# A hybrid decoder layer on one core: more products by the seven-product scheme, and an order of instructions worked out in rounds

## The chip, the core and the metric

The kernel runs on one NeuronCore of one Trainium2 chip. The metric is the device time of one launch in microseconds; of several runs the median is given. Engines: PE (TensorE, matrix products), DVE (VectorE), ACT (ScalarE), POOL (GpSimd, here mostly an issuer of accumulating DMAs), SP (SyncE, here the issuer of loads and stores), and 16 DMA engines behind all queues. PE writes into PSUM, which has 8 banks.

## What is computed

One layer for 256 tokens of width 2048, in float32, all weights read once from HBM:

```python
h = rmsnorm(x, g_mix); proj = h @ w_in            # 2048 x 15872
x_r, g_r, q, k, v, gate_r, gate_a = split(proj)   # 2816, 2816, then 2048 each
y_r = (gelu(g_r) * rg_lru(conv4(x_r))) @ w_rnn_out
y_a = stick_breaking_attention(norm(q), norm(k), v) @ w_attn_out   # 16 heads of 128
x = x + (sigmoid(gate_r) * y_r + sigmoid(gate_a) * y_a) @ w_o
g, u = split(rmsnorm(x, g_ffn) @ w_ffn_gu)        # 2 x 5632
x = x + (silu(g) * u) @ w_ffn_down
x = x + sigmoid(rmsnorm(x, g_ple) @ w_ple_gate) * (p @ w_ple_proj)
```

rg_lru is a gated linear recurrence over the tokens whose two gates come from 16 block-diagonal 176 x 176 products each.

## The kernel before, in words

**A product.** Every float32 operand is split into two float32r tiles, hi (a copy on ACT) and lo = value - hi (a subtraction on DVE), and `prod` (lines 202 to 214) runs three matmuls: hi x hi, hi x lo, lo x hi. Token tiles are the stationary side (128 x 128), weights the moving side (512 columns). A weight tile of 128 x 1024 (512 KB) is loaded by SP into `raw`, and `weights` makes `whi` and `wlo` of it.

**Groups.** `group` computes two blocks of 512 output columns for 256 tokens, over all k tiles of 128, in four PSUM banks (q). A plain k tile costs one weight tile and 4 products. Some k tiles are taken in pairs by a seven-product scheme (Strassen's, in Winograd's form): rows are the two k tiles of a pair, columns the two blocks of outputs, token halves the other side. Two pairs stand side by side in one tile, so a block of two pairs has seven weight tiles of 128 x 1024 ("11", "22", "21", and the sums T1 to T4) and 2 products for each, 14 where plain work has 4 weight tiles and 16 products. T1 = w11 + w12 and T3 = w22 + w12 are made by an accumulating DMA that POOL issues onto the raw tile (`add`), after its old content was split; T2 and T4 are added on DVE. Four of the seven go through a fifth bank (u), whose content is copied out by ACT (ja, jc, jd) and combined on DVE (je); at the end `join` adds those to the four banks. The token side needs, for each such pair, sums of its four quarters (`half_sums`: four small DVE operations and one split).

**Stages.** xr/gr in 6 groups (column blocks of the recurrent branch, with conv, gates, scan as hooks between k tiles of later groups), ro (2 groups), gtr, v, q and k, gta (gate of the attention branch), ao (attention output), wo, then the FFN: 11 gu groups and three rounds of dn over 16, 16 and 12 k tiles (order gu 0 to 3, dn, gu 4 to 7, dn, gu 8 to 10, dn), and pg (the last gate). The table `CFG` lists which pairs go by seven: 130 over all groups, none in ao.

**Gates.** `gates` (line 786 and on) puts the recurrence gate of two 128-column tiles into one PSUM bank, one half each, and the input gate's into another. ACT reads each half by a sigmoid as soon as the planner sees that half complete.

**The planner.** `build` records every operation with an engine, a duration, a latency and what it reads and writes; no instruction is issued yet. `deadlines` gives each a due time, back from the moment PE would use it. `schedule` then runs a clock over the five engines: among the ready operations PE takes the first in program order within a window of 60, the others the one due first, and each takes a buffer if there is one. There are 42 buffers of 128 x 1024 (L), 22 of 128 x 512 (H) and the 8 banks (P). A tile gets the buffer that has been free longest. The order of starts is the order in which `emit` writes the instructions; on the chip every engine runs its own list in that order, and semaphores hold true dependences.

Of the kernel before, what the change touches and what calls it, by code (L numbers as in the profile page):

```python
# [75 lines left out]
class Op:  # L76
    __slots__ = ("eng", "dur", "lat", "emit", "deps", "succ", "tiles", "due", "at", "n", "left", "ready",
                 "start", "table", "name", "cap", "acc", "reads", "size", "early")
# [9 lines left out]
class Program:  # L88
# [72 lines left out]
    def act(self, o, i, f, scale=None, bias=None, accum=None, name="", **kw):  # L161
        n = o.b - o.a
        reads, args = [i], {}
        for k, v in (("scale", scale), ("bias", bias)):
            if isinstance(v, Ref):
                reads.append(v)
        np_ = len(reads) - 1
        writes = [o] + ([accum] if accum is not None else [])

        def emit(nc):  # L170
            kw = {}
            for k, v in (("scale", scale), ("bias", bias), ("accum_out", accum)):
                if v is not None:
                    kw[k] = v.ap() if isinstance(v, Ref) else v
            nc.scalar.activation(o.ap(), i.ap(), f, **kw)  # L175
        d = 0.05 + 0.000875 * n + 0.09 * np_ + (0.2 if accum is not None else 0)
        return self.op("ACT", d, 0.15, emit, reads, writes, table=f, name=name, **kw)
# [60 lines left out]
LOAD_US, ADD_US, DMA_LEAD, DMA_TAIL = 1.575 / 512, 2.96 / 512, 1.3, 1.2  # L238
# [6 lines left out]
def deadlines(prog):  # L245
    for o in prog.ops:
        o.succ = []
    for o in prog.ops:
        for d in o.deps:
            d.succ.append(o)  # L250
    for o in reversed(prog.ops):
        if o.eng == "PE":
            o.due = o.at
            continue
        fin = o.at + (40.0 if o.cap is None else o.cap)
        if o.cap is None and any(r.t.kind == "P" for r in o.reads):
            fin = o.at + 2.5
        for s in o.succ:
            fin = min(fin, s.due)
        o.due = fin - o.lat - o.dur  # L260
        if o.size:
            o.due -= DMA_LEAD + DMA_TAIL + dma_us(o.size)


def schedule(prog, room, window, lag=0.0):
# [4 lines left out]
    deadlines(prog)  # L270
    for o in prog.ops:
        o.left = len(o.deps)
# [8 lines left out]
    free = {k: [(0.0, i) for i in range(n)] for k, n in room.items()}  # L281
# [31 lines left out]
    while left or events:  # L313
        moved = True
        while moved:
            moved = False
            for e in ready:
# [71 lines left out]
        while events and events[0][0] <= now + 1e-9:  # L389
# [7 lines left out]
            for t in o.tiles:  # L397
                t.left -= 1
                if t.left == 0 and t.kind in room:
                    heapq.heappush(free[t.kind], (now, t.slot))  # L400
    prog.span = now
    return sorted(prog.ops, key=lambda o: (o.start, o.n))

# [49 lines left out]
FQ = [16, 16, 12]  # L453


def order_of(ks, nd, lead=0):
# [7 lines left out]
    first, second = ("11", "22", "T1", "21"), ("T2", "T3", "T4")  # L464
    blocks = [[(m, d) for d in range(nd)] for m in (*first, *second)]
    n = len(ks)
    end = max(1, round(n / 7))
    rest = n - end
    out = blocks[0] + blocks[1]
    for i, b in enumerate(blocks[2:]):  # L470
        take = round(rest * (i + 1) / 5) - round(rest * i / 5)
        out += [ks.pop(0) for _ in range(take)]
        out += b
    return out + ks


def build(cfg):
# [31 lines left out]
    for n in ("h", "l"):  # L509
# [3 lines left out]
        w1t.append(t)  # L513

# [83 lines left out]
    def raw_of(tiles, name="raw"):  # L598
# [3 lines left out]
        return t, c  # L602

    def wslot(tiles):
        t, c = raw_of(tiles)
        return weights(t, c)
# [7 lines left out]
    def group(w, cols, ks, pairs, sums, tokens, how, hooks=None, lead=0):  # L614
# [16 lines left out]
        for n, x in enumerate(order):  # L631
# [10 lines left out]
            if m in ("11", "22", "21"):  # L642
                r, b = {"11": (0, 0), "21": (1, 0), "22": (1, 1)}[m]
                chain[m, dp] = raw_of(src(r, b, dp), "r" + m)[0]
# [3 lines left out]
            if m in ("T1", "T3"):  # L648
                if how(m) == "dma":
                    pr.add(raw.all, chain["b12", dp], 512, name="add")  # L650
                else:
# [4 lines left out]
            if m in ("T2", "T4"):  # L656
# [62 lines left out]


    xg, xsum = [], {}
    xp = cfg["x"]
# [63 lines left out]
    def gates(p):  # L786
# [31 lines left out]
        for e in range(2):  # L818
            s = slice(e * 256, e * 256 + 256)
            pr.vec(330, (lambda r, a, i: lambda nc: nc.vector.tensor_tensor_scan(r.ap(), a.ap(), i.ap(), 0.0, ALU.mult,  # L820
# [4 lines left out]
    def finish(p):  # L825
# [6 lines left out]
        if p in cfg["ro"]:  # L832
            ysum[p] = half_sums(r, "ys")

    def how(m):
        return "dma"

    def xr_group(b, n, hooks):
        c = [cols_of(C_XR + 4 * b, n), cols_of(C_GR + 4 * b, n)]
        if n == 4:  # L840
            out = group("in", c, range(KD), cfg["xr"][b], xsum, xg, cfg["how"], hooks, cfg["lead"] if b == 0 else 0)
# [75 lines left out]
    for g in range(2):  # L917
# [3 lines left out]
        for x in group("ro", c, range(KR), cfg["ro"], ysum, LazyPairs(y), cfg["how"], hooks):  # L921
# [9 lines left out]
    for g in range(2):  # L931
        c = [cols_of(C_GTR + 8 * g), cols_of(C_GTR + 8 * g + 4)]
        for n, x in enumerate(group("in", c, range(KD), cfg["gtr"], xsum, xg, cfg["how"])):
# [9 lines left out]
    for g in range(2):  # L943
        c = [cols_of(C_V + 8 * g), cols_of(C_V + 8 * g + 4)]
        for n, x in enumerate(group("in", c, range(KD), cfg["v"], xsum, xg, cfg["how"])):
# [7 lines left out]
    heads = {}  # L953
# [98 lines left out]
    def att_o(hp):  # L1052
# [16 lines left out]
        ost.append(split(ps.all, "ost"))  # L1069
# [24 lines left out]
    nq, ng = slots(KD, cfg["qk"]), slots(KD, cfg["gta"])  # L1094
    first = spread(att_hooks(range(4), cfg["att0"], cfg["every"], cfg["at"]), [nq, nq, ng, ng])
    second = spread(att_hooks(range(4, 8), cfg["att0"], cfg["every"], cfg["at"]), [ng, ng, 99])
# [5 lines left out]
    def qk(which, c0, g, hooks):  # L1102
        c = [cols_of(c0 + 8 * g), cols_of(c0 + 8 * g + 4)]
        head_norms(which, g, group("in", c, range(KD), cfg["qk"], xsum, xg, cfg["how"], hooks))
# [6 lines left out]
    for g in range(2):  # L1111
        c = [cols_of(C_GTA + 8 * g), cols_of(C_GTA + 8 * g + 4)]
        for n, x in enumerate(group("in", c, range(KD), cfg["gta"], xsum, xg, cfg["how"], hk[2 + g])):
# [9 lines left out]
    osum = {}  # L1123
    if cfg["ao"]:
        raise NotImplementedError
    mix, msum = {}, {}

    def next_mix(p):
        def run():
# [6 lines left out]
            if p in cfg["wo"]:  # L1136
# [15 lines left out]
    for g in range(2):  # L1152
        c = [cols_of(8 * g), cols_of(8 * g + 4)]
        for n, x in enumerate(group("ao", c, range(KD), cfg["ao"], osum, ost, cfg["how"], take(cfg["turn"]))):
# [34 lines left out]
    for g in range(2):  # L1189
        c = [cols_of(8 * g), cols_of(8 * g + 4)]  # L1190
        out = group("wo", c, range(KD), cfg["wo"], msum, mix, cfg["how"], take(cfg["turn"]))
# [7 lines left out]
        for p in range(4 * g, 4 * g + 4):  # L1199
            pend.append(next_h(hg, hsum, p, PC_GF, cfg["gu"], "hg"))  # L1200
# [7 lines left out]
    dn_pairs = {p for v in cfg["dn"] for p in v}  # L1208

    def gu(g):  # L1210
        c = [cols_of(4 * g), cols_of(44 + 4 * g)]
        out = group("gu", c, range(KD), cfg["gu"], hsum, hg, cfg["how"], take(cfg["turn"][:len(pend)]))
# [28 lines left out]
    def down(q, g):  # L1241
        c = [cols_of(8 * g), cols_of(8 * g + 4)]
        out = group("dn", c, range(f0[q], f0[q] + FQ[q]), cfg["dn"][q], asum, acts, cfg["how"],
# [6 lines left out]
        if q == len(FQ) - 1:  # L1250
            for p in range(4 * g, 4 * g + 4):
                pend.append(next_h(h3, sum3, p, PC_GP, cfg["pg"], "h3"))
# [14 lines left out]
    for g in range(2):  # L1267
        c = [cols_of(8 * g), cols_of(8 * g + 4)]
        out = group("pg", c, range(KD), cfg["pg"], sum3, h3, cfg["how"], take(cfg["turn"][:len(pend)]))
# [21 lines left out]
class LazyPairs:  # L1291


    def __init__(self, pairs):
        self.pairs = pairs

    def __getitem__(self, i):
        return self.pairs[i]
# [10 lines left out]
def make():  # L1309
    pr = build(CFG)  # L1310
    return pr, schedule(pr, ROOM, WINDOW)
# [78 lines left out]
```

## Time and profile before

| | |
|---|---|
| median of 3 runs | 1877.42 us (1877.06 to 1879.14) |
| the profiled execution | 1874.15 us |
| its span in the trace | 1872.4 us |
| PE, DVE, ACT busy | 98%, 86%, 68% of the span |
| loads, accumulating DMAs | 50.7%, 20.2% of 16 DMA engines' time |

How to read it: a wait is listed as *engine, waiting tile and line, <- engine and instruction that ended it: total us, times, longest*. A row of groups lists *line engine operation out<-in (shape) xcount | busy us, mean ns of one | idle before, releaser*. A stretch row gives *from:to, its length, then busy us (and count) of PE, PE's weight loads, DVE, ACT and POOL, the clock granted to PE, the mean share of the DMA engines that is busy, GB/s*. In a timeline "x6" merges six like instructions in a row, from the first one's start to the last one's end. A matmul's own duration overlaps the next one's; its spacing from start to start is what a product costs.

### The profile page before, as it was taken

The numbers are of one execution on the slowest core, as the hardware profiler recorded it, in microseconds if no ns is written. First come the engines' busy times: TensorE is split into PE (matmuls) and PEld (weight loads), VectorE is DVE, ScalarE is ACT, GpSimd is POOL, SyncE is SP. The second block draws the span as 40 slices with busy tenths as digits, with TensorE's granted clock in tenths as the row PEclk, the third lists the DMA queues.
The fourth block names the chain that finished last, engine by engine and source line by source line (L and its number), as shares of the span: only waits on it lengthen the run. The fifth ranks groups of instructions, "written<-read, shape, count | busy, mean of one in ns | idle before, by whom it ended". The sixth has DMA issues, their size and how long they took to land. (4 is left out here: it accounts for less than half of the span.)

```text
span 1872.4 us, 23719 instructions
## 1 busy us (share of the span) xinstructions
PE 1832.8 (98%) x8478; PEld 1523.6 (81%) x8478; DVE 1602.2 (86%) x1887; ACT 1277.0 (68%) x1696; POOL 115.5 (6%) x139
## 2 busy tenths in 40 slices
PE   8899999999999999999999999999999999999998
PEld 7678778888888888888888888888878888787887
DVE  7998998988888778888668889888898889898995
ACT  7798989856566677878645676666566656665773
POOL 0000000001000000000000000000100010000000
PEclk9999999999999999999999999999999999999999
DMA  9665665678877665656657777778877788777673
GB/s 368 199 188 184 191 186 177 190 238 262 240 229 230 206 191 162 188 170 236 205 168 221 221 205 206 200 217 243 262 202 205 225 220 265 209 215 246 194 226 103
DMA packets 112294, 397.52 MB, mean 212 GB/s; under 512 B 12592, under 2 KB 12976, under 8 KB 112176
## 3 DMA queue, kind: packets, MB, share of 16 engines
q1 hardware_dynamic: 93312, 327.84, 50.7%
q0 software_dynamic: 18720, 68.17, 20.2%
q8 instruction: 66, 1.08, 0.2%
q14 instruction: 52, 0.43, 0.1%
q10 hardware_dynamic: 144, 0.01, 0.0%
HBM read 393.86 MB, written 2.10 MB: 211 GB/s over the span
## 5 line engine op out<-in xcount | busy, mean ns | idle before, releaser
L175 ACT ACTIVATE shi<-r 128x1024 fp32r<-128x1024 f32 x455 | 472.7, 1054 | 250.6 <-DMA r<-in_w_dram 117.6
L142 DVE TENSOR_TENSOR slo<-r,shi 128x1024 fp32r<-128x1024 f32 x455 | 546.7, 1218 | 112.7 <-ACT shi L175 98.9
L142 DVE TENSOR_TENSOR wlo<-raw,whi 128x1024 fp32r<-128x1024 f32 (+2 forms) x418 | 499.7, 1206 | 60.8 <-ACT whi L175 49.5
L175 ACT ACTIVATE whi<-raw 128x1024 fp32r<-128x1024 f32 (+2 forms) x418 | 431.5, 1045 | 129.0 <-DMA raw<-in_w_dram 47.6
L210 PE MATMUL q<-whi,xg 128*128 128x512 f32 x624 | 245.4, 393 | 6.1 <-ACT xg L175 6.1
L211 PE MATMUL q<-wlo,xg 128*128 128x512 f32 x624 | 244.2, 391 | 2.5 <-DVE wlo L142 2.4
L212 PE MATMUL q<-whi,xg 128*128 128x512 f32 x624 | 243.9, 391 | 0.0
L188 POOL DMA_DIRECT2D r<-in_w_dram x130 | 113.4, 872 | 1704.3 <-DVE slo L142 853.0
L142 DVE TENSOR_TENSOR r<-r,r 128x1024 f32<-128x1024 f32 x130 | 157.9, 1219 | 1.2
L210 PEld LDWEIGHTS q<-whi,xg 128*128 128x128 f32 x624 | 117.8, 189 | 29.9 <-ACT xg L175 6.1
L211 PEld LDWEIGHTS q<-wlo,xg 128*128 128x128 f32 x624 | 117.8, 189 | 27.3 <-DVE wlo L142 3.6
L210 PE MATMUL q<-whi,hg 128*128 128x512 f32 x352 | 139.0, 395 | 0.0
L211 PE MATMUL q<-wlo,hg 128*128 128x512 f32 x352 | 138.1, 392 | 0.0
L212 PE MATMUL q<-whi,hg 128*128 128x512 f32 x352 | 137.8, 392 | 0.0
L212 PEld LDWEIGHTS q<-whi,xg 128*128 128x128 f32 x624 | 117.7, 189 | 24.7
L212 PEld LDWEIGHTS q<-whi,hg 128*128 128x128 f32 x352 | 66.8, 190 | 14.1
L211 PEld LDWEIGHTS q<-wlo,hg 128*128 128x128 f32 x352 | 66.8, 190 | 13.7
L210 PEld LDWEIGHTS q<-whi,hg 128*128 128x128 f32 x352 | 66.7, 190 | 13.6
L210 PE MATMUL q<-whi,act 128*128 128x512 f32 x192 | 75.6, 394 | 0.0
L211 PE MATMUL q<-wlo,act 128*128 128x512 f32 x192 | 74.9, 390 | 0.0
L212 PE MATMUL q<-whi,act 128*128 128x512 f32 x192 | 74.8, 390 | 0.0
L175 ACT ACT_TABLE_LOAD x52 | 66.7, 1283 | 2.2 <-PEq L1377 1.2
(412 smaller groups left out, 3719.0 us busy)
## 6 DMA issues: line engine op xcount, KB each, us to landing
raw<-in_w_dram SPq DMA_DIRECT2D x396, 512.0 KB, 4.5
r<-in_w_dram SPq DMA_DIRECT2D x195, 512.0 KB, 4.7
r<-in_w_dram POOLq DMA_DIRECT2D x130, 512.0 KB, 7.5
raw<-in_w_dram SPq DMA_DIRECT2D x16, 448.0 KB, 4.0
xq<-in_x_dram SPq DMA_DIRECT2D x8, 256.0 KB, 8.0
x<-in_x_dram SPq DMA_DIRECT2D x8, 256.0 KB, 6.7
xt<-in_xT_dram SPq DMA_DIRECT2D x7, 256.0 KB, 8.4
raw<-in_w_dram SPq DMA_DIRECT2D x4, 320.0 KB, 4.9
```

The lines of the kernel that those rows point to most:

```text
L142: return self.vec(n, lambda nc: nc.vector.tensor_tensor(o.ap(), a.ap(), b.ap(), op), [a, b], [o], name=name, **kw)
L175: nc.scalar.activation(o.ap(), i.ap(), f, **kw)
L188: return self.op("POOL", 0.85, 0.0, lambda nc: nc.gpsimd.dma_start(o.ap(), src(nc), accum_op=ALU.add), [], [o], size=-kb, name=name)
L210: nc.tensor.matmul(ps.ap(), x[0].ap(), w[0].ap(), start=start, stop=False, **kw)
L211: nc.tensor.matmul(ps.ap(), x[0].ap(), w[1].ap(), start=False, stop=False, **kw)
L212: nc.tensor.matmul(ps.ap(), x[1].ap(), w[0].ap(), start=False, stop=stop, **kw)
```

## The change

1. `CFG`: 184 pairs by seven instead of 130. gtr and v go from 4 pairs to 6 a group, q, k and gta from 2 to 4, ao from 0 to 4, wo from 2 to 4, ten of the gu groups from 4 to 6, the second pg group from 4 to 6. In q, k, gta and ao T4 too is made by an accumulating DMA (from w21, read again) instead of DVE. Token sums are made for the pairs that any group uses; the attention output gets a copy (h) for it.
2. `order_of`: the seven-product steps are spread differently among the plain k tiles.
3. In a PSUM bank an operation of another engine now depends on all recorded PE operations on the bank, whatever half they touch, and the other way round.
4. Nine matmuls on constants (warm) ahead of the first product.
5. A load issued by SP takes the buffer freed last; all else the one free longest, as before.
6. The planner's costs: ACT's are split by PSUM and SBUF source, the scan's is raised, loads are due 5 us earlier, and data counts as seen 0.5 us (loads) or 2 us (accumulating DMAs) later.
7. `improve` runs `schedule` 20 times. After each it looks, for every gap of PE in its own clock, back along the chain that ended last, and makes those operations due earlier by up to 3 us. The order of the round with the shortest planned run is used.

```diff
-                    if overlap(a, b, r.a, r.b):
+                    if overlap(a, b, r.a, r.b) or (t.kind == "P" and (eng == "PE") != (p.eng == "PE")):
...
-                        t.slot = heapq.heappop(free[t.kind])[1]
+                        if o.eng == "SP":
+                            i = max(range(len(free[t.kind])), key=lambda i: free[t.kind][i][:2])
+                        else:
+                            i = 0
+                        _, t.slot, o.why = free[t.kind].pop(i)
...
-                    seen = server + DMA_TAIL
+                    seen = server + DMA_TAIL + (LATE if o.size < 0 else LATE / 4)
...
+def improve(prog, room, window, rounds, gain=1.0):
+    boost, best, kept = {}, None, {}
+    for _ in range(rounds):
+        order = schedule(prog, room, window, boost)
+        if best is None or prog.span < best:
+            best, kept = prog.span, dict(boost)
...
+            x, n = o, 0
+            while x is not None and n < 40:
+                d = max(x.deps, key=lambda d: (d.start + d.dur + d.lat, d.n), default=None)
+                if d is None or d.start + d.dur + d.lat < x.start - 0.6:
+                    d = x.why if x.why is not None else d
+                if d is None or d.eng == "PE":
+                    break
+                add[d.n] = max(add.get(d.n, 0.0), min(gap, 3.0))
+                x, n = d, n + 1
+        for n, v in add.items():
+            boost[n] = boost.get(n, 0.0) + gain * v
+    order = schedule(prog, room, window, kept)
+    return order
...
+    cuts = [round(n * f) for f in SPREAD]
+    p = [ks[i:j] for i, j in zip([0] + cuts, cuts + [n])]
+    s = {m: [(m, d) for d in range(nd)] for m in ("11", "22", "T1", "21", "T2", "T3", "T4")}
+    h = (nd + 1) // 2
+    return (s["11"] + s["22"] + p[0] + s["T1"] + s["21"][:h] + p[1] + s["T2"] + s["21"][h:] + p[2] + s["T3"] + p[3]
+            + s["T4"] + p[4])
...
+    warm = tile("warm", "P")
+    pr.mms([(warm.all, ones_r.all, w1t[0].all, 0.4, True, True) for _ in range(9)], [ones_r.all, w1t[0].all], [warm.all],
+           name="warm")
+    pr.pe = 0.0
...
-CFG = dict(lead=8, x=[4, 5, 6, 7], xr=[[6, 7]] + [[4, 5, 6, 7]] * 4, ro=[0, 1, 2, 3], gtr=[4, 5, 6, 7], v=[4, 5, 6, 7], qk=[4, 5], gta=[4, 5],
-           ao=[], wo=[0, 1], gu=[0, 1, 2, 3], dn=[[0, 1, 2, 3], [8, 9, 10, 11], [16, 17]], pg=[0, 1, 2, 3],
-           how=lambda m: "dma", att0=4, every=9, at=(0, 4, 10, 16), turn=[4, 5, 6, 7])
+F4, F6, X4, X6 = [0, 1, 2, 3], [0, 1, 2, 3, 4, 5], [4, 5, 6, 7], [2, 3, 4, 5, 6, 7]
+LATER = ("T1", "T3", "T4")
+CFG = dict(xr=[[6, 7]] + [X4] * 4, ro=[F4] * 2, gtr=[X6] * 2, v=[X6] * 2, qk=[X4] * 4, gta=[X4] * 2, ao=[F4] * 2,
+           wo=[F4] * 2, gu=[F4] + [F6] * 10, dn=[[F4] * 2, [[8, 9, 10, 11]] * 2, [[16, 17]] * 2], pg=[F4, F6],
+           how=dict(qk=LATER, gta=LATER, ao=LATER), lead=8, att0=4, every=9, at=(0, 4, 10, 16), turn=[4, 5, 6, 7])
```

The program that comes out has 162 matmuls of products fewer and the nine warming ones more, 27 loads fewer (621 DMAs of SP instead of 648) and 70 accumulating DMAs more (200 instead of 130).

More of the change, by code (lines that the diff above doesn't have):

```diff
@@ L77 @@
     __slots__ = ("eng", "dur", "lat", "emit", "deps", "succ", "tiles", "due", "at", "n", "left", "ready",
-                 "start", "table", "name", "cap", "acc", "reads", "size", "early")
+                 "start", "why", "table", "name", "cap", "acc", "reads", "size", "early")
 def overlap(a, b, c, d):
@@ L175, in emit @@
             nc.scalar.activation(o.ap(), i.ap(), f, **kw)
-        d = 0.05 + 0.000875 * n + 0.09 * np_ + (0.2 if accum is not None else 0)
+        d = (0.03 + 0.000875 * n if i.t.kind == "P" else 0.094 + 0.000832 * n) + 0.09 * np_ + (0.13 if accum is not None else 0)
         return self.op("ACT", d, 0.15, emit, reads, writes, table=f, name=name, **kw)
@@ L261, in deadlines, with schedule @@
         if o.size:
-            o.due -= DMA_LEAD + DMA_TAIL + dma_us(o.size)
-def schedule(prog, room, window, lag=0.0):
+            o.due -= DMA_LEAD + DMA_TAIL + SPARE + dma_us(o.size)
+        if boost:
+            o.due -= boost.get(o.n, 0.0)
+def schedule(prog, room, window, boost=None):
     import bisect
     import heapq
-    deadlines(prog)
+    deadlines(prog, boost)
     for o in prog.ops:
-        o.left = len(o.deps)
+        o.left, o.why = len(o.deps), None
     wait = {}
@@ L280, in schedule @@
         wait[k].sort()
-    free = {k: [(0.0, i) for i in range(n)] for k, n in room.items()}
+    free = {k: [(0.0, i, None) for i in range(n)] for k, n in room.items()}
     pes = [o for o in prog.ops if o.eng == "PE"]
@@ L399, in schedule @@
                 if t.left == 0 and t.kind in room:
-                    heapq.heappush(free[t.kind], (now, t.slot))
+                    bisect.insort(free[t.kind], (now, t.slot, o), key=lambda x: x[:2])
     prog.span = now
     return sorted(prog.ops, key=lambda o: (o.start, o.n))
+def improve(prog, room, window, rounds, gain=1.0):
[4 more added lines that the diff above has]
+            best, kept = prog.span, dict(boost)
+        end = 0.0
+        add = {}
+        for o in order:
+            if o.eng != "PE":
+                continue
+            gap = o.start - end
+            end = o.start + o.dur
+            if gap < 0.05:
+                continue
+            x, n = o, 0
[11 more added lines that the diff above has]
+    return order
 def emit(prog, order, nc, tc, pools):
@@ L453 @@
 FQ = [16, 16, 12]
+SPREAD = (0.3, 0.5, 0.65, 0.8)
 def order_of(ks, nd, lead=0):
@@ L463, in order_of @@
         return ks[:lead] + order_of(ks[lead:], nd)
-    first, second = ("11", "22", "T1", "21"), ("T2", "T3", "T4")
-    blocks = [[(m, d) for d in range(nd)] for m in (*first, *second)]
     n = len(ks)
[L467 to L474, printed above, removed]
+    cuts = [round(n * f) for f in SPREAD]
[4 more added lines that the diff above has]
+            + s["T4"] + p[4])
 def build(cfg):
@@ L601, in raw_of @@
         pr.load(t[:c], src, c // 2, name=name)
-        return t, c
+        return t, src
     def wslot(tiles):
-        t, c = raw_of(tiles)
-        return weights(t, c)
+        return weights(raw_of(tiles)[0], P * len(tiles))
     def part(w, a, n):
@@ L647, in group @@
             raw = chain["22" if m in ("22", "T3") else "21" if m == "21" else "11", dp]
[L648 to L651, printed above, removed]
+            if m in how:
+                s_ = {"T1": "b12", "T3": "b12", "T2": "b22", "T4": "b21"}[m]
+                pr.add(raw.all, chain[s_, dp], 512, name="add")
+            elif m in ("T1", "T3"):
+                if True:
                     if ("r12", dp) not in chain:
@@ L718, in token_scales, with hw, union @@
         rsqrt_mean(r.all, v[:2], D)
+    def hw(stage, g):
+        h = cfg["how"].get(stage, ("T1", "T3"))
+        return h[g] if isinstance(h, list) else h
     xg, xsum = [], {}
-    xp = cfg["x"]
+    def union(*keys):
+        return sorted({p for k in keys for v in cfg[k] for p in v})
+    xp = union("xr", "gtr", "v", "qk", "gta")
     for i in range(NPD):
@@ L831, in finish @@
         y.append(split(r.all, "y"))
-        if p in cfg["ro"]:
+        if p in union("ro"):
             ysum[p] = half_sums(r, "ys")
-    def how(m):
-        return "dma"
     def xr_group(b, n, hooks):
@@ L840, in xr_group @@
         if n == 4:
-            out = group("in", c, range(KD), cfg["xr"][b], xsum, xg, cfg["how"], hooks, cfg["lead"] if b == 0 else 0)
+            out = group("in", c, range(KD), cfg["xr"][b], xsum, xg, hw("xr", b), hooks, cfg["lead"] if b == 0 else 0)
             for i, x in enumerate(out):
@@ L920, in build @@
                           (8, lambda: finish(8)), (11, lambda: finish(9)), (15, finish_last)]) if g == 0 else None
-        for x in group("ro", c, range(KR), cfg["ro"], ysum, LazyPairs(y), cfg["how"], hooks):
+        for x in group("ro", c, range(KR), cfg["ro"][g], ysum, y, hw("ro", g), hooks):
             if x[1] is None:
@@ L932, in build @@
         c = [cols_of(C_GTR + 8 * g), cols_of(C_GTR + 8 * g + 4)]
-        for n, x in enumerate(group("in", c, range(KD), cfg["gtr"], xsum, xg, cfg["how"])):
+        for n, x in enumerate(group("in", c, range(KD), cfg["gtr"][g], xsum, xg, hw("gtr", g))):
             o = join(x, "gt")
@@ L944, in build @@
         c = [cols_of(C_V + 8 * g), cols_of(C_V + 8 * g + 4)]
-        for n, x in enumerate(group("in", c, range(KD), cfg["v"], xsum, xg, cfg["how"])):
+        for n, x in enumerate(group("in", c, range(KD), cfg["v"][g], xsum, xg, hw("v", g))):
             o = join(x, "v")
@@ L950, in build @@
             vs.append(v)
-    heads = {}
+    heads, osum = {}, {}
     qs, ks_, zst, ost = {}, {}, {}, []
@@ L1068, in att_o @@
         pr.mms(jobs, reads, [ps.all], name="o")
-        ost.append(split(ps.all, "ost"))
+        if hp in union("ao"):
+            h = tile("h", "H")
+            act(h.all, ps.all, AF.Copy, name="h")
+            ost.append(split(h.all, "ost"))
+            osum[hp] = half_sums(h, "os")
+        else:
+            ost.append(split(ps.all, "ost"))
     steps = (att_t, att_z, att_e, att_o)
@@ L1092, in slots @@
         return nk - 2 * len(pairs) + 7 * (len(pairs) // 2)
-    nq, ng = slots(KD, cfg["qk"]), slots(KD, cfg["gta"])
-    first = spread(att_hooks(range(4), cfg["att0"], cfg["every"], cfg["at"]), [nq, nq, ng, ng])
-    second = spread(att_hooks(range(4, 8), cfg["att0"], cfg["every"], cfg["at"]), [ng, ng, 99])
+    nq, ng = [slots(KD, v) for v in cfg["qk"][2:]], [slots(KD, v) for v in cfg["gta"]]
+    first = spread(att_hooks(range(4), cfg["att0"], cfg["every"], cfg["at"]), nq + ng)
+    second = spread(att_hooks(range(4, 8), cfg["att0"], cfg["every"], cfg["at"]), ng + [99])
     hk = [first[0], first[1], first[2], first[3], {}]
@@ L1102, in qk @@
     def qk(which, c0, g, hooks):
+        n = 2 * g + (which == "k")
         c = [cols_of(c0 + 8 * g), cols_of(c0 + 8 * g + 4)]
-        head_norms(which, g, group("in", c, range(KD), cfg["qk"], xsum, xg, cfg["how"], hooks))
+        head_norms(which, g, group("in", c, range(KD), cfg["qk"][n], xsum, xg, hw("qk", n), hooks))
     qk("q", C_Q, 0, None)
@@ L1112, in build @@
         c = [cols_of(C_GTA + 8 * g), cols_of(C_GTA + 8 * g + 4)]
-        for n, x in enumerate(group("in", c, range(KD), cfg["gta"], xsum, xg, cfg["how"], hk[2 + g])):
+        for n, x in enumerate(group("in", c, range(KD), cfg["gta"][g], xsum, xg, hw("gta", g), hk[2 + g])):
             o = join(x, "ga")
@@ L1153, in build @@
         c = [cols_of(8 * g), cols_of(8 * g + 4)]
-        for n, x in enumerate(group("ao", c, range(KD), cfg["ao"], osum, ost, cfg["how"], take(cfg["turn"]))):
+        for n, x in enumerate(group("ao", c, range(KD), cfg["ao"][g], osum, ost, hw("ao", g), take(cfg["turn"]))):
             o = join(x, "ya")
@@ L1190, in build @@
         c = [cols_of(8 * g), cols_of(8 * g + 4)]
-        out = group("wo", c, range(KD), cfg["wo"], msum, mix, cfg["how"], take(cfg["turn"]))
+        out = group("wo", c, range(KD), cfg["wo"][g], msum, mix, hw("wo", g), take(cfg["turn"]))
         for n, x in enumerate(out):
@@ L1207, in build @@
     f0 = [sum(FQ[:q]) for q in range(len(FQ))]
-    dn_pairs = {p for v in cfg["dn"] for p in v}
+    dn_pairs = {p for v in cfg["dn"] for u in v for p in u}
     def gu(g):
         c = [cols_of(4 * g), cols_of(44 + 4 * g)]
-        out = group("gu", c, range(KD), cfg["gu"], hsum, hg, cfg["how"], take(cfg["turn"][:len(pend)]))
+        out = group("gu", c, range(KD), cfg["gu"][g], hsum, hg, hw("gu", g), take(cfg["turn"][:len(pend)]))
         sg = []
@@ L1242, in down @@
         c = [cols_of(8 * g), cols_of(8 * g + 4)]
-        out = group("dn", c, range(f0[q], f0[q] + FQ[q]), cfg["dn"][q], asum, acts, cfg["how"],
+        out = group("dn", c, range(f0[q], f0[q] + FQ[q]), cfg["dn"][q][g], asum, acts, hw("dn", q),
                     take(cfg["turn"][:len(pend)]))
@@ L1268, in build @@
         c = [cols_of(8 * g), cols_of(8 * g + 4)]
-        out = group("pg", c, range(KD), cfg["pg"], sum3, h3, cfg["how"], take(cfg["turn"][:len(pend)]))
+        out = group("pg", c, range(KD), cfg["pg"][g], sum3, h3, hw("pg", g), take(cfg["turn"][:len(pend)]))
         gate = []
```

28 lines of the change are left out of this document (10 added, 18 removed).

## The prediction

> **What bounds the kernel now.** First the head of the page, then what TensorE (PE) waits for, then busy time stretch by stretch.
>
> ```profile
> span 1872.4 us, 23719 instructions
> ...
> PE 1832.8 (98%) x8478; PEld 1523.6 (81%) x8478; DVE 1602.2 (86%) x1887; ACT 1277.0 (68%) x1696; POOL 115.5 (6%) x139
> ```
> PE has work in 98% of the span, VectorE (DVE) in 86%. So the number of products sets the time, and DVE is next in line.
>
> ```profile
> PE rg L799 <- ACT rr L175: 12.0, 9, 3.7
> PE q L210 <- ACT xg L175: 6.1, 1, 6.1
> PE gut L221 <- DVE jc L146: 5.4, 2, 2.8
> PE rg L799 <- ACT ri L175: 2.8, 5, 0.6
> PE u L210 <- ACT ja L175: 2.7, 1, 2.7
> PE q L211 <- DVE wlo L142: 2.4, 1, 2.4
> PE u L211 <- DVE slo L142: 2.0, 3, 1.3
> PE gut L221 <- DVE jd L146: 0.5, 2, 0.3
> ```
> This is the whole list of PE's waits (total us, times, longest): 33.9 us. 14.8 us are gate products (rg) held by ScalarE (ACT) reading the other half of their bank; 6.1 us is the first load; 8.6 us are late reads at the ends of FFN groups (gut, ja); only 4.4 us are weight halves (wlo, slo) that DVE had not finished, and no wait is for a DMA.
>
> Busy time by stretch (us; PE, PEld, DVE, ACT, POOL with counts; granted clock; DMA share; GB/s): first the opening 312 us, then the stretches that matter below.
>
> ```profile
> 0.00:312.00 312.00, 287.25 (x1418) 239.76 (x1419) 281.43 (x403) 263.69 (x363) 19.78 (x29) 0.99 0.70 217
> ```
> ```profile
> 222.50:276.60 54.10, 51.65 (x264) 43.31 (x263) 51.43 (x71) 46.74 (x65) 1.72 (x2) 1.00 0.66 206
> ...
> 439.00:520.00 81.00, 81.00 (x359) 67.07 (x359) 72.04 (x72) 52.02 (x58) 7.84 (x9) 1.00 0.84 242
> 520.00:602.00 82.00, 82.00 (x363) 67.94 (x362) 70.77 (x72) 53.06 (x60) 6.10 (x7) 1.00 0.73 221
> 602.00:686.00 84.00, 84.00 (x372) 69.57 (x371) 64.17 (x69) 51.16 (x90) 3.48 (x4) 1.00 0.70 212
> ...
> 1237.00:1320.00 83.00, 83.00 (x372) 68.73 (x371) 74.94 (x77) 49.63 (x53) 6.96 (x8) 1.00 0.80 234
> 1320.00:1491.00 171.00, 168.00 (x745) 138.55 (x744) 148.76 (x161) 107.68 (x122) 13.94 (x16) 0.99 0.76 219
> ```
> From 439 on PE is full; almost all loss is in the first 312 us, where DVE is 281.43/312 = 90% busy too.
>
> **Part 1, the products.** A pair of k tiles costs 8 products plain and 7 by the scheme; a product is 3 matmuls. 54 more pairs (130 to 184) drop 162 matmuls. At 81.00 us for 359 (row 439) one takes 0.226 us: **-36.6 us**, all on the path. What comes in their place lies on other engines:
>
> ```profile
> 904.60 6.89 DVE L142 TENSOR_TENSOR wlo<-raw,whi 128x1024 fp32r<-128x1024 f32 x6
> ```
> ```profile
> 903.21 4.84 ACT L175 ACTIVATE whi<-raw 128x1024 fp32r<-128x1024 f32 x5
> ```
> ```profile
> L142 DVE TENSOR_TENSOR je<-jd,je 128x512 f32<-128x512 f32 x38 | 26.0, 684 | 11.0 <-ACT jd L175 10.9
> ...
> L142 DVE TENSOR_TENSOR hs<-h 128x128 f32<-128x128 f32 x48 | 12.4, 283 | 6.9 <-ACT h L175 6.8
> ...
> L142 DVE TENSOR_TENSOR as<-hs,as 128x512 fp32r<-128x512 f32 x10 | 6.9, 685 | 0.5 <-ACT as L175 0.5
> ```
> Back to back, one 1024-wide DVE operation takes 6.89/6 = 1.15 us, one ACT copy 4.84/5 = 0.97. Each of the 27 new blocks of two pairs has 7 weight tiles for 4: +81 copies and +81 lo parts. T2 and T4 are DVE sums: +54, less 16 where T4 becomes an accumulating DMA (q/k, gta, ao): +38. 119 x 1.15 = 137 us. Two ao groups now join (12 x 0.68 = 8 us), 12 more pairs need token half sums (4 x 0.28 + 0.69 = 1.8 each, 22 us). DVE: 1602 + 168 = **1770 us**. ACT gains 81 x 0.97 and some 16 of small ones: 1277 + 95 = 1372, three quarters of the span, no bound.
>
> **Where DVE then exceeds PE.** A gtr, v or gu group loses 2 products (6 x 0.226 = 1.36 us of PE) and gains 5 wide DVE operations (5.75 us). Rows 439 and 520: DVE 72.04 + 11.5 = 83.5 against PE 81 - 2.7 = 78.3, and 82.3 against 79.3: over by 5.2 and 3.0. Row 1320 (four gu groups): 148.76 + 23 = 171.8 against 168 - 5.4 = 162.6: over by 9. But row 602 (q, k: T4 by DMA, so 3 operations more a group, 3.45 us) stays at 71.1 against 81.3, and row 1237 (dn, unchanged) at 74.94 against 83. The tight stretches alternate with slack ones, so it matters how far DVE may run ahead:
>
> ```profile
> SPq L182 <- PE q L212: 759.7, 241, 16.5
> ```
> ```profile
> ACT whi L175 <- PE q L212: 39.2, 29, 3.8
> ```
> Loads wait mostly for PE to give a buffer back, and so do the splits at times: the buffers are full ahead of PE, and PE found a weight late only 4 times in all. New waits cost between 0 and 42 us (the second rival); I take **+3**, near the lower end, since rows 439 to 602 ran at 88% DVE with no PE wait.
>
> **Part 2, gates read when complete.** The sigmoids now follow the last product of the whole bank. What that wait holds behind it is ACT's queue: weight copies, which the new order puts ahead. It can save 14.8 us and one clock dip, and at worst hand back everything (the bank stays occupied longer, 0):
>
> ```profile
> 6.10:11.60 5.50, 5.41 (x12) 3.93 (x13) 4.84 (x8) 4.37 (x6) 0.00 (x0) 1.00 0.99 393
> ...
> 190.00:199.30 9.30, 5.60 (x34) 4.85 (x33) 9.30 (x17) 8.63 (x12) 0.86 (x1) 1.00 0.76 163
> 199.30:202.80 3.50, 3.50 (x19) 3.50 (x18) 2.19 (x3) 1.42 (x2) 0.00 (x0) 0.51 0.48 154
> ...
> 1711.40:1714.90 3.50, 3.50 (x12) 2.79 (x11) 3.03 (x3) 3.50 (x5) 0.00 (x0) 0.51 0.65 263
> ```
> After the longest stalls the granted clock is 0.51 for 3.5 us, 1.7 us lost; four such in the run. So the gates' upper value is 16.5 us. What is late next is DVE: 281.4 us in the first 312, and 5 us more for two more pairs of x. At the share of row 222 (51.43/54.10 = 95%, the highest of a long stretch) 286 us need 301, so some 11 us can be had of this region.
>
> **Part 3, nine warming products.** The first q products take 5.41/12 = 0.45 us each until 11.6, twice the later 0.226: half speed, whatever the clock column says there. Full speed from 6.1 would save 12 x 0.226 = 2.7 us, if weights came as fast; with the DMA share 0.99 there I take 1.5 (0 to 2.7). The products run before the first weights land, in PE's idle 6.1 us; 9 x 0.45 = 4.1 us fit. Parts 2 and 3 together: **-12**.
>
> [...]
>
> **Part 4, the order in 20 rounds, newest buffers, new planner costs.** They cost no instruction. The rounds move what PE waited for earlier. The FFN's three stalls (8.6 us in gut and ja, three dips 5.1) are worth 0 to 13.7; I take **-5**, since DVE is fuller there than now. Loads into the newest free buffer wait on the instruction that freed it last, with all later loads behind them on SP's queue; the oldest buffers are left for ACT and DVE. 0, inside the bounds of the new waits.
>
> **Sum.** 1872.4 - 36.6 - 12 - 5 + 3 = 1821.8 us of span. The profiled execution took 1874.15, 1.75 more than its span; the median of the runs is 1877.42, 5.0 more. Forecast **1827 us**.
>
> **Rivals.**
> *No wait left.* 33.9 - 6.1 = 27.8 us of waits, 6.8 of dips, 2.7 of start go: 1872.4 - 36.6 - 37.3 = 1798.5, so 1803 or less. Against it: DVE would have to be 98% busy.
>
> *DVE becomes the bound.* If it cannot be kept fuller than 95% (row 222), 1770/0.95 = 1863, with the 5.0: **1868**. For it: the excesses above, and DVE's idle share would fall from 14% to 3%. Against it: row 222 lies where PE stood at the gates, and a PE that stands leaves DVE without free buffers.
>
> *The DMA engines become the bound: slower.*
>
> ```profile
> q1 hardware_dynamic: 93312, 327.84, 50.7%
> q0 software_dynamic: 18720, 68.17, 20.2%
> ```
> ```profile
> r<-in_w_dram SPq DMA_DIRECT2D x195, 512.0 KB, 4.7
> r<-in_w_dram POOLq DMA_DIRECT2D x130, 512.0 KB, 7.5
> ```
> A 512 KB load takes 0.507 x 1872.4 x 0.524/327.84 = 1.52 us of the 16 engines, an accumulating one 0.202 x 1872.4/130 = 2.91. 27 loads go, 70 adds come: +163, 82% of the new span. From 439 to 686: 68 + 60 + 59 = 187 us now; +4.3 for each of four groups, +10.1 for each of two: 224 in 239, 94%. A gu group asks 13 x 1.52 + 6 x 2.91 = 37.2 in 40.3, an ao group 38.7 in some 41.7. Together these ask 673 us in 725. Rows with adds show at most 0.84: if that were the limit, 673/0.84 - 725 = 76 us more, **1903**. It makes the kernel slower than now from 0.87 down (51 us). Against it: 0.99 in row 6.10, though with loads alone, and PE never waited for a DMA.
>
> [...]
>
> ```profile
> L188 POOL DMA_DIRECT2D r<-in_w_dram x130 | 113.4, 872 | 1704.3 <-DVE slo L142 853.0
> ```
> [...]
>
> **How the numbers follow.** A measurement tells 0.2% (3.8 us) from no change. Forecast, 1802 to 1848: 0.60. No wait left, below 1802: 0.06. DVE the bound, 1848 to 1873: 0.18; its far end within 0.2%: 0.03. DMA the bound, above 1881: 0.13. Faster 0.84, same 0.03, slower 0.13. The range 1800 to 1872 holds the first, most of the third and a little of the second, about 0.8.
>
> **What would show it.** Products: 8325 matmuls, PE busy some 35 us less. Gates: the rr and ri waits gone from PE's list. Warming: products at 0.23 us spacing from the first q on. DVE: busy near 1770; if it is the bound, PE waits for wlo and slo reach tens of us, above all from 439 to 602 and in the gu groups. DMA: ACT waits for r grow and PE waits through shi. The forecast is wrong if PE's waits after 312 us come to more than some 25 us, or if the first 312 us shrink by less than 5.

## The result, and the profile after

The changed kernel takes **1820.73 us** (median of 4 runs, 1819.43 to 1822.80) against 1877.87 for the kernel before in the same runs: ratio 0.9696, 95% interval 0.9679 to 0.9713. The forecast was 1827. The profiled execution took 1822.80 us, with a span of 1821.1 us where 1821.8 was forecast.

The head of the page after:

```profile
span 1821.1 us, 24029 instructions
...
PE 1797.6 (99%) x8325; PEld 1489.7 (82%) x8325; DVE 1742.5 (96%) x2076; ACT 1351.9 (74%) x1803; POOL 176.3 (10%) x209
...
q1 hardware_dynamic: 89424, 313.68, 49.0%
q0 software_dynamic: 28800, 104.87, 31.6%
...
r<-in_w_dram SPq DMA_DIRECT2D x276, 512.0 KB, 5.3
r<-in_w_dram POOLq DMA_DIRECT2D x200, 512.0 KB, 7.7
```

PE is busy 35.2 us less, DVE 140 us more: it is now 96% busy beside a PE at 99%. The DMA engines are 81% busy. PE's waits, the whole list:

```profile
PE q L211 <- DVE slo L142: 7.5, 7, 3.1
PE u L211 <- DVE slo L142: 4.1, 5, 2.1
PE q L211 <- DVE wlo L142: 3.3, 6, 0.8
PE warm L199 <- DVE one L534: 1.6, 1, 1.6
PE q L210 <- ACT whi L175: 0.7, 1, 0.7
PE rg L847 <- DVE xcs L142: 0.2, 1, 0.2
```

The gates' waits (14.8 us) and those at the ends of the FFN groups (8.6 us) are gone. What is left is new in kind: 14.9 us in which PE waits for a lo part, where it was 4.4. The stretches show why. First the opening, where the kernel before had 1418 matmuls done, then stretches chosen for what follows:

```profile
0.00:312.00 312.00, 303.24 (x1523) 255.19 (x1524) 295.24 (x430) 274.37 (x385) 19.61 (x29) 0.99 0.73 225
```
```profile
413.00:570.00 157.00, 157.00 (x695) 129.99 (x694) 152.64 (x149) 104.39 (x115) 20.04 (x23) 1.00 0.92 251
1038.00:1206.00 168.00, 166.99 (x750) 136.53 (x749) 168.00 (x194) 120.44 (x151) 19.14 (x22) 1.00 0.81 219
...
1288.00:1455.00 167.00, 164.07 (x725) 134.47 (x724) 164.66 (x177) 114.19 (x130) 20.04 (x23) 0.99 0.84 232
1536.00:1658.00 122.00, 122.00 (x547) 100.98 (x547) 120.93 (x127) 84.31 (x96) 13.95 (x16) 1.00 0.88 243
```
In gtr and v (413 to 570) the DMA engines are 92% busy and PE loses nothing. In gu 0 to 3 (1038 to 1206) DVE is busy 168.00 of 168.00, and PE stands 1.0 us; in gu 4 to 7 (1288 to 1455) DVE is busy 164.66 of 167.00, and PE stands 2.9 us.

### The profile page after: what moved, and what is told of

The parts are those of the page before. It is cut to its first block, busy times and chain, and to the rows that moved or that the text cites. A ratio compares the mean times of both kernels' runs of the same rounds, so it can differ in the third digit from the quotient of the medians.

```text
span 1821.1 us, 24029 instructions
## 1 busy us (share of the span) xinstructions
PE 1797.6 (99%) x8325; PEld 1489.7 (82%) x8325; DVE 1742.5 (96%) x2076; ACT 1351.9 (74%) x1803; POOL 176.3 (10%) x209
## 5 line engine op out<-in xcount | busy, mean ns | idle before, releaser
L175 ACT ACTIVATE shi<-r 128x1024 fp32r<-128x1024 f32 x644 | 659.2, 1053 | 233.5 <-DVE r L142 93.2
L142 DVE TENSOR_TENSOR slo<-r,shi 128x1024 fp32r<-128x1024 f32 x644 | 774.4, 1239 | 22.5 <-ACT shi L175 20.8
L142 DVE TENSOR_TENSOR wlo<-raw,whi 128x1024 fp32r<-128x1024 f32 (+2 forms) x310 | 375.5, 1219 | 17.2 <-ACT whi L175 11.1
L175 ACT ACTIVATE whi<-raw 128x1024 fp32r<-128x1024 f32 (+2 forms) x310 | 318.9, 1040 | 49.6 <-PE q L211 15.5
L210 PE MATMUL q<-whi,xg 128*128 128x512 f32 x464 | 182.7, 394 | 0.7 <-ACT whi L175 0.7
L212 PE MATMUL q<-whi,xg 128*128 128x512 f32 x464 | 181.1, 390 | 0.0
L211 PE MATMUL u<-slo,hgs 128*128 128x512 f32 x192 | 75.8, 395 | 2.9 <-DVE slo L142 2.9
L211 PE MATMUL u<-slo,xs 128*128 128x512 f32 x198 | 77.9, 394 | 0.6 <-DVE slo L142 0.6
L210 PE MATMUL u<-shi,xs 128*128 128x512 f32 x198 | 78.1, 395 | 0.0
L212 PE MATMUL u<-shi,xs 128*128 128x512 f32 x198 | 77.7, 392 | 0.0
L210 PE MATMUL u<-shi,hgs 128*128 128x512 f32 x192 | 75.7, 394 | 0.0
L212 PE MATMUL u<-shi,hgs 128*128 128x512 f32 x192 | 75.5, 393 | 0.0
L210 PE MATMUL q<-whi,hg 128*128 128x512 f32 x192 | 74.9, 390 | 0.0
```

What stands on the lines that cost most here:

```text
L142: return self.vec(n, lambda nc: nc.vector.tensor_tensor(o.ap(), a.ap(), b.ap(), op), [a, b], [o], name=name, **kw)
L210: nc.tensor.matmul(ps.ap(), x[0].ap(), w[0].ap(), start=start, stop=False, **kw)
L211: nc.tensor.matmul(ps.ap(), x[0].ap(), w[1].ap(), start=False, stop=False, **kw)
L212: nc.tensor.matmul(ps.ap(), x[1].ap(), w[0].ap(), start=False, stop=stop, **kw)
```

## The experiments

Each kernel was compared with the kernel before on its own chip. That kernel's median moved from 1874.3 to 1878.5 us between the chips, so a difference of a few us between two kernels of different chips is not told by their medians alone; the ratios go by the pair.

**1. What else but the products? The order alone, and the bank rule alone.** `pairs_130` is the kernel after with the pairs of before (its table is shortened here):

```diff
-gtr=[X6] * 2, v=[X6] * 2, qk=[X4] * 4, gta=[X4] * 2, ao=[F4] * 2, wo=[F4] * 2, gu=[F4] + [F6] * 10, pg=[F4, F6], how=dict(...)
+gtr=[X4] * 2, v=[X4] * 2, qk=[[4, 5]] * 4, gta=[[4, 5]] * 2, ao=[[]] * 2, wo=[[0, 1]] * 2, gu=[F4] * 11, pg=[F4] * 2, how={}
```

> The kernel after with the 130 pairs of before; all else of the change is kept. Theory: PE has 36.6 us more to do and DVE's late weight halves (some 15 us) mostly go: 1842 to 1858 us. Rival, that the order in rounds makes most of the gain: 1835 us or less.

1843.64 us, ratio 0.9842 (0.9826 to 0.9857): in the theory's range. But read from before, the order alone (changes 2 to 7 together) is worth 30.7 us, and the 54 pairs on top of it bring 23 us by the medians, 27 by the ratios, 22 by the spans, not 36.6: from pairs_130 (span 1842.9, PE busy 1828.7) to the kernel after PE is busy 31.1 us less and idle 9.3 us longer. `before_gate` is the kernel before with one line:

```diff
-if overlap(a, b, r.a, r.b):
+if overlap(a, b, r.a, r.b) or (t.kind == "P" and (eng == "PE") != (p.eng == "PE")):
```

> The kernel before with the bank rule alone (an operation of another engine on a PSUM bank depends on all PE operations there). Theory: the gates' waits are worth what the trace after shows, some 16 us between 105 and 312 us, whatever else is changed: 1859 to 1864 us. Rival: DVE, 90% busy in the first 312 us, takes the place of the gates, and 10 us or less are had: 1867 us or more.

1859.78 us, ratio 0.9927 (0.9902 to 0.9953), in the theory's range; the span is 1856.4 for 1872.4. PE's four longest waits:

```profile
PE gut L221 <- DVE jc L146: 6.2, 2, 4.0
PE q L210 <- ACT xg L175: 5.9, 1, 5.9
PE u L211 <- DVE slo L142: 3.3, 5, 1.3
PE rg L801 <- DVE wlo L142: 2.9, 2, 1.7
```
No gate product waits for ACT any more; the FFN's stalls at gut stay. So the rule makes about half of what the order gives. DVE does not hold it back in the opening as the rival had it: by 312 us this kernel has 1498 matmuls done where the kernel before had 1418, and its last gate product starts at 321.0 us instead of 334.9.

**2. The 184 pairs alone.** `products_alone` is the kernel after with change 1 only (`schedule` once, old costs, old spreading, oldest buffers, no bank rule, no warming).

> The kernel before with the 184 pairs alone (old planner, old costs, old spreading, no bank rule, no warming). Theory: the 36.6 us of PE work go, the gates' and FFN stalls stay and DVE adds up to 15 us of waits: 1841 to 1856 us. Rival: without the 20 rounds DVE's load turns into PE waits and eats most of the gain: 1862 us or more.

1909.97 us, ratio **1.0198** (1.0174 to 1.0222): slower than before by 36 us, far beyond both. PE has 162 matmuls fewer, but it is busy only 9.2 us less (1823.6), at a mean granted clock of 0.987 where it was 0.996, and idle 46.3 us longer. PE's longest waits, then ACT's for landing tiles and DVE's for ACT:

```profile
PE q L211 <- DVE wlo L142: 20.5, 18, 5.7
PE rg L842 <- ACT rr L175: 12.8, 9, 2.0
PE u L210 <- ACT jc L175: 9.7, 7, 2.2
PE q L210 <- ACT whi L175: 9.6, 4, 3.9
PE q L211 <- DVE slo L142: 6.3, 5, 1.6
PE u L211 <- DVE slo L142: 5.9, 9, 1.9
```
```profile
ACT shi L175 <- DMA r<-in_w_dram: 200.1, 108, 6.7
```
```profile
DVE slo L142 <- ACT shi L175: 82.8, 70, 5.9
```
The same two rows of the kernel before:

```profile
ACT shi L175 <- DMA r<-in_w_dram: 117.6, 56, 6.5
```
```profile
DVE slo L142 <- ACT shi L175: 98.9, 76, 6.1
```
DVE is not full with the pairs alone (91%); it stands 83 us for ACT, which stands 200 us for tiles that have not landed. In the kernel before both stood like this too, DVE even longer, while PE waited only 4.4 us for lo parts and for no DMA, so its list was silent on this. What differs is the idle time of DVE: 270 us of the span before, 164 here. That late data reach PE by way of ACT and DVE once DVE has too little idle time to make up for it fits these rows; that the planner's timing of the data is most of the cause, experiment 3 shows.

With pairs_130 this makes a table of four. Changes 2 to 7 are worth 31 us with 130 pairs and 89 with 184; the 54 pairs cost 36 us under the old order and bring 22 to 27 under the new one.

**3. Which part of the planner carries the pairs?** Two parts added to the pairs alone. `p_margin` adds the two DMA margins (the line is shortened, the remark is not in the kernel):

```diff
-SPARE, LATE = 0.0, 0.0
+SPARE, LATE = 5.0, 2.0   # loads due 5 us earlier; data seen 2 us (adds) or 0.5 us (loads) later
```

> The kernel with the 184 pairs alone (1910 us) plus the planner's two DMA margins and nothing else. Theory data: late data is most of what sank the 184 pairs alone; ACT's waits for landing tiles fall from 200 us to some 100: 1860 to 1888 us. Rival: the margins are worth the 15 us that their removal cost the kernel after: 1892 us or more.

1846.41 us, ratio 0.9849 (0.9833 to 0.9864): **64 us** for two constants, past the theory's own range. The same two rows:

```profile
ACT shi L175 <- DMA r<-in_w_dram: 76.9, 45, 4.8
```
```profile
DVE slo L142 <- ACT shi L175: 26.9, 30, 1.8
```
Both fall to about a third. `p_rounds` adds the 20 rounds instead (and holds the products of a gate bank in program order by one more dependence, marked "order" below):

```diff
-return pr, schedule(pr, ROOM, WINDOW)
+return pr, improve(pr, ROOM, WINDOW, 20)
...
+                if w in seen:          # "order"
+                    o.deps.add(seen[w])
+                seen[w] = o
```

> The kernel with the 184 pairs alone (1910 us) plus the 20 rounds, on the old costs (and the gate products of a bank kept in program order on PE). Theory data: a plan made better by its own clock stays wrong where that clock is wrong, 1895 us or more. Rival: rounds and margins stand in for each other, either rescues the order: 1880 us or less.

1881.88 us, ratio 1.0037 (1.0019 to 1.0055): between the two, 1.9 us above the rival's, 28 us better than the pairs alone, and ACT still stands 195.6 us for landing tiles. Rounds help, but on a clock that is wrong about the data they do not rescue the pairs. What "order" does by itself was not measured, here or in the kernels below that have it.

**4. One part of the planner taken out of the kernel after.** `old_lead` sets the margins to zero, `one_round` runs `schedule` once, `oldest_f` gives loads the buffer free longest, `old_spread_f` has the old `order_of` (the last two with "order"):

```diff
-LOAD_US, ADD_US, DMA_LEAD, DMA_TAIL, SPARE, LATE = 1.575 / 512, 2.96 / 512, 1.3, 1.2, 5.0, 2.0
+LOAD_US, ADD_US, DMA_LEAD, DMA_TAIL, SPARE, LATE = 1.575 / 512, 2.96 / 512, 1.3, 1.2, 0.0, 0.0
```


> The kernel after with the planner's two new DMA margins back at zero (loads due 5 us earlier; data seen 0.5 or 2 us later). The kernel with the 184 pairs alone had ACT waiting 200 us for landing tiles (74 after) and DVE 83 us for ACT (21 after). Theory data: the margins are what lets the 184 pairs run, and without them PE's waits for weight halves return: 1845 us or more. Theory rounds: the 20 rounds are what counts, and this costs 12 us or less: 1833 us or less.

`old_lead`: 1835.51 us, ratio 0.9780 (0.9759 to 0.9800): between the two, nearer the lower; ACT's wait for r tiles is back at 184 us (74 after), but the rounds keep PE from most of it.

> The kernel after with one pass of the planner instead of 20 rounds. Theory rounds: PE's waits return, 1845 us or more. Theory data: the rounds only mend single places, the stalls at the ends of FFN groups among them: 1822 to 1833 us.

`one_round`: 1825.46 us, ratio 0.9726 (0.9707 to 0.9745), in the range of the theory on data.

> The kernel after with loads taking the buffer free longest, as before, and the gate products of a bank kept in program order on PE. Theory: which buffer a load takes is worth little, since a plan that holds has it free when the load is due: 1818 to 1828 us. Rival: newest buffers leave the old ones to ACT and DVE and so let them run ahead; without it 1835 us or more.

`oldest_f`: 1825.67 us, ratio 0.9724 (0.9702 to 0.9747), as the theory had it.

> The kernel after with the seven-product steps spread among the plain tiles as before, and the gate products of a bank kept in program order on PE. Theory: the spread moves DVE's work by a few us inside a group, no more: 1819 to 1830 us. Rival: with up to three blocks in a group the old spread puts too many wide DVE operations side by side and PE waits in all gu groups: 1838 us or more.

`old_spread_f`: 1825.36 us, ratio 0.9725 (0.9707 to 0.9744), as the theory had it. These three medians stand some 5 us above the kernel after, on another chip, and the intervals overlap with its own (0.9679 to 0.9713): none of the three parts is told from nothing by itself. Margins and rounds stand in for each other in part: added to the pairs alone, the margins are worth 64 us and the rounds 28; taken out of the kernel after, 15 and some 5.

**5. The warming products.** `no_warm` leaves them out:

```diff
-    warm = tile("warm", "P")
-    pr.mms([(warm.all, ones_r.all, w1t[0].all, 0.4, True, True) for _ in range(9)], [ones_r.all, w1t[0].all], [warm.all],
-           name="warm")
-    pr.pe = 0.0
```


> The kernel after without the nine warming products. Theory: DVE and the loads, not the clock, set the first 60 us, so the time stays within 2 us: 1819 to 1823 us. [...]

1821.10 us, ratio 0.9724 (0.9709 to 0.9739), its span 1819.0. By the medians, on two chips, that is 0.4 us from the kernel after, as the theory had it; by the ratios it is some 5 us slower, with intervals that overlap (0.9709 to 0.9739, 0.9679 to 0.9713). So the times do not settle what sets the first 60 us, and the traces have to tell. The opening of the kernel after, then without warming:

```profile
6.00:11.00 5.00, 4.23 (x16) 2.92 (x17) 4.55 (x6) 4.23 (x7) 1.02 (x1) 1.00 0.94 339
...
60.00:105.00 45.00, 41.23 (x186) 33.88 (x186) 43.40 (x62) 36.84 (x49) 3.46 (x4) 0.92 0.71 209
0.00:105.00 105.00, 96.48 (x413) 77.22 (x414) 97.00 (x159) 84.83 (x124) 9.18 (x17) 0.97 0.84 274
```
```profile
6.00:11.00 5.00, 4.46 (x10) 3.18 (x11) 4.29 (x5) 3.58 (x7) 1.02 (x1) 1.00 0.97 344
...
60.00:105.00 45.00, 41.20 (x199) 34.10 (x198) 44.69 (x66) 38.59 (x52) 3.46 (x4) 1.00 0.78 215
0.00:105.00 105.00, 93.75 (x414) 76.14 (x415) 97.99 (x161) 85.97 (x126) 9.21 (x17) 1.00 0.87 277
```
Warming does bring the first products forward: with it PE does 16 matmuls from 6 to 11 us (0.23 us apart from 7.50 to 10.05), without it 10 (4.46 us busy, 0.45 each), at a granted clock of 1.00 in both rows. But both kernels have issued the same 279 matmuls of products when they come to the same lo part, the kernel after at 73.5 us and the one without warming at 73.9, and both stand for it. After, then without warming:

```profile
77.00 0.79 PE L211 MATMUL q<-slo,xg 128*128 128x512 f32 x1 [3.12 <-DVE slo L142]
```
```profile
77.50 0.50 PE L211 MATMUL q<-slo,xg 128*128 128x512 f32 x1 [3.16 <-DVE slo L142]
```
So 0.5 us of the lead is left there: DVE sets the time, as the theory said, and not the clock. By 105 us the kernel without warming has done 414 matmuls, the kernel after 413 with the nine of warming, 10 products fewer. That comes from what follows the stall: in the kernel after the granted clock falls to 0.51 from 77.0 to 83.05 us, in the other it does not fall (0.92 and 1.00 in the rows from 60 to 105). Since both stood equally long, this fall is not shown to be due to warming.

**6. Is DVE what is left?** `gu_t4b` takes 11 wide sums from DVE in the gu groups and gives the DMA engines 11 adds more; `w2` relieves DVE in the opening too:

```diff
-            if m in how:
+            if m in how or (m, dp) in how:
...
-           how=dict(qk=LATER, gta=LATER, ao=LATER), ...
+           how=dict(qk=LATER, gta=LATER, ao=LATER, gu=("T1", "T3", ("T4", 0))), ...          # gu_t4b
+           how=dict(..., gu=("T1", "T3", ("T4", 0)), xr=LATER), xr=[[6, 7], [6, 7]] + [X4] * 3, ...   # w2, with "order" and 40 rounds
```


> The kernel after with one of two or three T4 sums of each gu group made by an accumulating DMA instead of DVE (11 wide DVE operations fewer, 11 adds more). Theory DVE: the waits at the ends of the gu triples come from a DVE that is 100% busy there, and mostly go, 8 us of excess: 1811 to 1817 us. Rival: the DMA engines, then asked for 40.1 of each 40.3 us in a gu group, turn into the bound: 1825 us or more.

1812.30 us, ratio 0.9666 (0.9652 to 0.9681), in the theory's range. Stretches of gu_t4b that hold gu 0 to 3, 4 to 7 and 8 to 10:

```profile
1030.00:1190.00 160.00, 160.00 (x727) 132.56 (x726) 160.00 (x197) 115.89 (x145) 20.88 (x24) 1.00 0.87 236
...
1270.00:1440.00 170.00, 169.60 (x758) 139.53 (x757) 169.44 (x182) 118.28 (x135) 24.41 (x28) 1.00 0.93 252
1520.00:1650.00 130.00, 130.00 (x583) 107.69 (x582) 128.34 (x136) 89.13 (x102) 18.30 (x22) 1.00 0.96 264
```
PE's standing in gu 0 to 3 and 4 to 7 is gone but for 0.4 us, with DVE still full and the DMA engines at 87 to 96%. At 0.96 with adds in the mix PE lost nothing in 130 us.

> The same, and DVE relieved in the first 300 us as well: T4 by DMA in the xr groups, two pairs instead of four in the second xr group (1.4 us more PE work), 40 rounds, gate products in program order. Theory DVE: the 12 us lost in the first 105 us partly go too: 1803 to 1813 us. Rival: the first 60 us are set by the loads and the rest is as in the kernel with the gu sums alone: the same as that within 2 us, or slower.

1810.01 us, ratio 0.9651 (0.9637 to 0.9666), in the theory's range. It and gu_t4b are the fastest of all runs, 1808.63 to 1814.13 us against 1819.43 to 1822.80 for the kernel after on another chip; by the ratios w2's interval lies below that of the kernel after, and gu_t4b's (0.9652 to 0.9681) just touches it. Between the two, 2.3 us stand inside their intervals. In the traces the last gate product starts at 315.7 us in w2 and at 318.5 in gu_t4b; what the edits to the opening bring by themselves, without the 40 rounds and "order", stays open.

## Why the forecast held, point by point

**The total** held within 1 us of span and 6.3 us of time. The 5.0 us added for median over span did not repeat: the profiled run after was the slowest of its four. But several terms were off and made up for each other. Up to the last gate product the kernel after is 16.2 us ahead of the kernel before (318.7 for 334.9 us), where gates and warming were put at 12; from there to the end it gains 35.1 where 38.6 were forecast (36.6 + 5 - 3). One part came out 4.2 us better, the other 3.5 worse; that the span was met within 1 us is luck.

**Products: right on PE, wrong as a term of its own.** 8325 matmuls and PE busy 35.2 us less, as said. The sum put -36.6 "all on the path" and gave the planner's new costs 0, since "they cost no instruction". That step failed: the pairs alone are 36 us slower than before, and two constants for late data are worth 64. The forecast was right since the change brings both together. The numbers were there to be seen. By its old constants the planner had a load's data at the earliest 1.3 + 1.575 + 1.2 = 4.1 us after issue and an add's 1.3 + 2.96 + 1.2 = 5.5, while the page of before gave 4.7 and 7.5 as medians; with the margins it is 4.6 and 7.5. Which of the two margins, LATE or the earlier due time, does the most was not tried apart.

**Gates: mechanism right, size too small.** With warming they were put at 12 us, held to that by a DVE that could not pass 95%. The bank rule alone took 14.5 us by the medians and 16.0 of span, close to the upper value of 16.5; 13.9 us of that are had by the last gate product. The share of 95% was not passed there: up to the last gate product DVE is busy 93% with the bank rule alone and 94% after. What was set too high is DVE's work, 286 us with 5 for two more pairs of x: in that same stretch DVE is busy 299.1 us before and 299.8 after, not 5 more.

**Warming: 0.5 us left by 77 us** where 1.5 was taken and 2.7 was the upper end. That matmuls on constants would bring q's first products to 0.23 us was the author's assumption, which no row of before shows; the runs show 16 matmuls from 6 to 11 us with them and 10 without. The reason given for taking less (the loads) points the right way: both kernels stood for the same lo part. What is left of it in the whole time is not told by the runs.

**FFN stalls and new waits: two errors of one size.** The old stalls went wholly (13.7 with their dips, 5 was taken). New waits came to more than the 3 us taken: PE's waits for lo parts grew by 10.5 us, and two stalls brought dips. Of the 14.9 us, the stretches named for them (439 to 602 and the gu groups) hold 5.4; 6.2 lie in the first 105 us, which were not named. Experiment 6 shows that DVE makes those in the gu groups.

**Rivals.** That no wait is left (1803 us or less) did not come true: 17.4 us of PE's waits remain. DVE as the bound of the whole (1868 us) did not come true: its 95% was no limit, as stretches at 100% show; in gu 0 to 3 and 4 to 7 it was the bound, at a price of some 8 us by the medians of gu_t4b and 6 by the ratios. Its load came out at 1742.5 us, not 1770, though the count of its operations is as forecast: the trace's DVE records overlap where they stand close (they add up to 1722 us in 1602 busy before, to 1938 in 1742.5 after), so packing them takes busy time off the old ones as well. The DMA engines as the bound (1903 us) are refuted by rows at 0.92 and 0.96 with PE full. Their delay was the danger, not their rate: products_alone is slower than before with engines at 77% (46.8% loads, 30.4% adds). POOL's issuing was no limit either: an add's issue takes it 872 ns before and after, and after it is busy 176.3 us in all. The forecast looked for "PE waits through shi" only as a sign of full engines.

## What to carry to other kernels

An order planned ahead is only as good as its clock: compare the planner's time from issue to landing with the page's, for each kind of transfer, before judging what a change of load will do. Here the new order was worth 31 us with DVE at 86% and 89 with the pairs that bring DVE to 96%, so work shifted onto an engine that is nearly full has to be judged together with the order. When two engines are both nearly full, look for stretches at 100% of the second one, and move a little of its work there to a third.

## What was not expected of the hardware

The 16 DMA engines held 0.96 for 130 us, half of it accumulating DMAs (22 issues at about 2.9 us of all engines each, an estimate: 33.9% of gu_t4b's span of 1812.4 us over its 211 adds), without a wait of PE. Half-speed stretches of PE (a granted clock of 0.50 to 0.51) follow some stalls and not others. The stall of 3.1 to 3.2 us near 75 us is followed by 6.8 us at half speed in the kernel after (a mean granted clock of 0.62 from 75 to 84), by some 3.4 in gu_t4b (0.89 from 75 to 90) and by none without warming; one of 2.1 us, which ends at 1433.6 us in the kernel after, is followed by 3.4 (0.50 from 1434.6 to 1438.0). In the kernel after:

```profile
75.00:84.00 9.00, 7.00 (x20) 5.57 (x21) 9.00 (x12) 3.71 (x6) 0.00 (x0) 0.62 0.28 101
```
A late weight can thus cost more than its own length: from 77.0 us on 14 matmuls take 6.05 us, where at 0.226 us each they would take 3.2, so 2.9 us come on top of the 3.1 of standing. What decides whether the clock falls after a stall, no run here shows.
